# A table of attention biases written 16 times instead of 128, read by eight transfers, and compressor weights asked for in two pieces

## The chip, the cores and the metric

The kernel runs on one core of a Trainium2 chip. The metric is the time of one execution on the device in microseconds, the median of several runs. One further execution was recorded by the hardware profiler; its rows are shown below.

The core has a matrix engine (TensorE, PE in the rows, with its weight loads as PEld), VectorE (DVE), ScalarE (ACT), GpSimd (POOL) and SyncE (SP), and sixteen DMA engines that all transfers share. Each engine takes its instructions in order and waits on semaphores. SP, ACT and POOL also issue transfers; SP's and ACT's go through hardware queues (q1, q10 in the rows), POOL's through a software queue (q0).

## The reference

One layer of a block: normalise, project to many heads, two kinds of attention, project back, normalise, a feed-forward network. Only the part around the change is shown.

```
h = rms_norm(x, norm_mix_pre);  proj = h @ w_in            # x: 512 x 2048, all float32
k_cmp = compress_kv(kv6[:, :, 0], pe_k, w1_k, b1_k, w2_k)  # 31 blocks of 32 tokens, step 16
v_cmp = compress_kv(kv6[:, :, 1], pe_v, w1_v, b1_v, w2_v)
o_a = nsa_attention(q_a, k_cmp, v_cmp, k_slc, v_slc, k_win, v_win, gates, t5_bias)
o_r = silu(g_r) * retention(rope(q_r), rope(k_r), v_r)
x = x + rms_norm(concat(o_a, o_r) @ w_out);  x = x + rms_norm(square(relu(rms_norm(x) @ w_up)) @ w_down)

def compress_kv(kv, pe, w1, b1, w2):                       # w1: (32*128) x 128
    flat = (blocks of kv + pe).reshape(n_cmp, 32 * 128)
    return gelu(flat @ w1 + b1) @ w2
# in nsa_attention, for each of 8 heads, before each softmax:
s = q @ k.T * scale + t5_table[bucket(t_query - t_key), head]
```

The bias depends on the distance between query and key and on the head alone. So one row of 640 values for each head holds all of it, and the biases of query p are that row shifted by p places.

## The kernel before, in words

All products are made from two-part operands: ScalarE rounds a float32 tile to a high part (`whi`), VectorE subtracts to get the low part (`wlo`), and three matmuls (lines 154 to 156) add up. Weights come in slabs of 256 rows and up to 512 columns: SP asks for a slab (`raw`, line 175, three buffers), ScalarE casts it (line 143), VectorE subtracts (line 144), and TensorE uses it for 24 matmuls. There are three buffers for raw slabs and three for the two parts. Blocks of columns of `w_in` follow one another, eight slabs each: first the early value columns, then the **kv block** (the keys and values that are compressed), the **k block** (two transfers for each slab), the query block of the first group, and so on. `Driver.run` writes the casts of a slab two slabs ahead of its use, and its order in the program is the order on every engine.

Beside the products runs other work, cut into steps by generators: after some products `side.step()` takes one step of it. In the kv, k and first query blocks one step follows every second column group (`two`), so two for each slab. The first three units are `bias_table`, `compress(0)` for keys and `compress(1)` for values; the attention units (`nsa_unit`) of the first group follow from the fourth block on.

`bias_table` makes the table: two small matmuls give `rsb`, 8 heads on 8 partitions with 640 values each. POOL then writes it to DRAM as `rd`, with every head's row repeated 128 times (line 458). `load_bias` (line 551) reads it back for four heads of a group into `BT`: partition p takes row p at an offset of 127 - p, which gives the shift. One transfer does it, since a step of one row less one value moves on by a row and back by a place. The first load is written after the first query block, the second at the end of the first group's attention. `BT` is added to scores on VectorE (lines 572 and 582).

`compress(i)` asks on SP for the position rows `pes`, the bias `b1s`, `w2s` and the two halves of w1 (`w1s`, 16 x 128 x 128 values each, 1.05 MB, line 492); two steps later it transposes `pes` (L496), copies it beside the keys or values (`KV`, L497 on ScalarE), and runs 32 matmuls in four steps (L501): the first two read the first half of w1, the last two the second. The small transfers wait until the other compressor has read its own, since they share buffers.

Buffers are named by tags. `rsb`, `hot` and the two `KV` tiles share a tag with two buffers, so the third and fourth copies into `KV` (line 479) wait until the write of `rd` has read `rsb` to the end. `w1s` and `BT` share the tag `big`.

Of the kernel before, what the change touches and what calls it, by code (L numbers as in the profile page):

```python
# [10 lines left out]
F32 = mybir.dt.float32  # L11
# [5 lines left out]
P = 128  # L17
S = 512
# [4 lines left out]
HA, NG, DK = 8, 2, 128  # L23
# [3 lines left out]
EPS = 1e-6  # L27
KC = 2
NSLAB = KT // KC
RD = 639  # L30
LAST = 384

OFF_KV = HA * DK
# [79 lines left out]
def block_kernel(ctx: ExitStack, tc: tile.TileContext, x, norm_mix_pre, w_in, cmp_pe_k, cmp_w1_k, cmp_b1_k,  # L113
                 cmp_w2_k, cmp_pe_v, cmp_w1_v, cmp_b1_v, cmp_w2_v, t5_bias, w_out, norm_mix_post, norm_mlp_pre,
                 w_up, w_down, norm_mlp_post, c_rot, c_dec, c_hot, c_misc, out):
    nc = tc.nc
# [8 lines left out]
    dram = ctx.enter_context(tc.tile_pool(name="dram", bufs=1, space=bass.MemoryType.DRAM))  # L125
# [15 lines left out]
    def split(hi, lo, src):  # L141

        nc.scalar.copy(hi, src)  # L143
        nc.vector.tensor_sub(lo, src, hi.bitcast(F32))  # L144
# [18 lines left out]
    def bank(tag, bufs=1):  # L163
        return pp.tile([P, S], F32, name=tag, tag=tag, bufs=bufs)
# [140 lines left out]
    ap = actx.enter_context(tc.tile_pool(name="att", bufs=1))  # L305
# [140 lines left out]
    nc.gpsimd.dma_start(g3r, norm_mlp_pre.rearrange("o (k p) -> (o k) p", p=P))  # L446
    rot = rp.tile([P, 2, S], F32, name="rot")
    nc.gpsimd.dma_start(rot, c_rot)
    rd = dram.tile([HA, P, RD], F32, name="rd")

    def bias_table():
        rsb = ap.tile([HA, 640], F32, name="rsb", tag="P", bufs=2)
        for c0, n in ((0, 512), (512, 128)):
            ps = bank("S")
            nc.tensor.matmul(ps[:HA, :n], tbl, hot[:, c0:c0 + n], start=True, stop=True)
            nc.vector.tensor_copy(rsb[:, c0:c0 + n], ps[:HA, :n])
            yield
        nc.gpsimd.dma_start(rd, rsb[:, None, :RD].to_broadcast([HA, P, RD]))
        pt = bank("PT", 2)
        nc.tensor.transpose(pt[:, :KT], g3r, ident[:KT, :KT])  # L460
        nc.vector.tensor_copy(g3T, pt[:, :KT])
        yield
# [18 lines left out]
    def compress(i):  # L481
        pe, w1, b1, w2 = ((cmp_pe_k, cmp_w1_k, cmp_b1_k, cmp_w2_k), (cmp_pe_v, cmp_w1_v, cmp_b1_v, cmp_w2_v))[i]
        kv = KV[i]
        pes = ap.tile([CBLK, DK], F32, name="pes")
        nc.sync.dma_start(pes, pe[0])
        b1s = ap.tile([DK, 2], F32, name="b1s")
        nc.sync.dma_start(b1s[:, 0:1], b1.rearrange("o n -> n o"))
        w2s = ap.tile([DK, DK], F32, name="w2s")
        nc.sync.dma_start(w2s, w2[0])
        w1s = [ap.tile([P, 16, DK], F32, name="w1s", tag=("qT", "big")[c]) for c in range(2)]  # L490
        for c in range(2):
            nc.sync.dma_start(w1s[c], w1[0][c * 16 * P:(c + 1) * 16 * P, :].rearrange("(l p) n -> p l n", p=P))
        yield
        yield
        pt = bank("PT", 2)
        nc.tensor.transpose(pt[:, :CBLK], pes, ident[:CBLK, :CBLK])  # L496
        nc.scalar.copy(kv[:, NG * S:], pt[:, :CBLK])  # L497
        yield
        hid = bank("oT")
        for l in range(CBLK):  # L500
            nc.tensor.matmul(hid[:65, :DK], kv[:, l:l + STRIDE * 64 + 1:STRIDE], w1s[l // 16][:, l % 16, :],  # L501
                             start=l == 0, stop=l == CBLK - 1)
            if l % 8 == 7:
                yield
        hs = ap.tile([65, DK], F32, name="hs")
        nc.scalar.copy(hs, hid[:65, :DK])
        yield
        pt = bank("PT", 2)
        nc.tensor.transpose(pt[:, :65], hs, ident[:65, :65])
        nc.vector.tensor_add(b1s[:, 1:2], b1s[:, 0:1], pt[:, 64:65])  # L510
        z = ap.tile([DK, 4, 63], F32, name="z")
        nc.vector.tensor_scalar_add(z[:, 0, :], pt[:, :63], b1s[:, 1:2])

        nc.vector.tensor_mul(z[:, 1, :], z[:, 0, :], z[:, 0, :])
        nc.vector.tensor_scalar(z[:, 1, :], z[:, 1, :], 0.044715, 1.0, op0=ALU.mult, op1=ALU.add)
        nc.vector.tensor_mul(z[:, 1, :], z[:, 1, :], z[:, 0, :])
        nc.scalar.activation(z[:, 2, :], z[:, 1, :], AF.Exp, scale=-2.0 * float(np.sqrt(2.0 / np.pi)))
        yield
        nc.vector.tensor_scalar_add(z[:, 2, :], z[:, 2, :], 1.0)
        nc.vector.reciprocal(z[:, 2, :], z[:, 2, :])  # L520
        nc.vector.tensor_mul(z[:, 3, :], z[:, 0, :], z[:, 2, :])
        yield
        o = bank("PT", 2)
        if i == 0:
            nc.tensor.matmul(o[:, :63], w2s, z[:, 3, :], start=True, stop=True)
            for g in range(NG):
                nc.vector.tensor_copy(kS[:, g, :NCMP], o[:, g * 32:g * 32 + NCMP])
        else:
            for g in range(NG):
                nc.tensor.matmul(o[:NCMP, g * DK:(g + 1) * DK], z[:, 3, g * 32:g * 32 + NCMP], w2s,  # L530
                                 start=True, stop=True)
            split(vch, vcl, o[:NCMP, :NG * DK])
        yield

    QT, BT = {}, {}
# [12 lines left out]

    def load_bias(g):
        BT[g] = ap.tile([P, 4, S], F32, name="BT", tag="big")  # L550
        nc.gpsimd.dma_start(BT[g], bass.AP(tensor=rd.tensor, offset=rd.offset + g * 4 * P * RD + P - 1,
                                           ap=[[RD - 1, P], [P * RD, 4], [1, S]]))

    def nsa_unit(g, i, pr):

# [6 lines left out]
        def scores():  # L562
# [40 lines left out]
            if g == 0 and i == NT - 1 and pr == 1:  # L603
                load_bias(1)
# [170 lines left out]
    three = lambda c: side.step() if c else None  # L775
    after = lambda n: (lambda: drv.at > n * B)
    side.add(bias_table, nothing)
    side.add(lambda: compress(0), nothing, after(1))
    side.add(lambda: compress(1), nothing, after(1))
    for u in range(8):  # L780
        side.add(*nsa_unit(0, u // 2, u % 2), after(3), after(4))
# [7 lines left out]
    for blocks, units, firsts, pump in ((3, 3, 0, two), (4, 0, 0, two), (7, 10, 11, three), (8, 11, 12, three),  # L789
                                        (9, 12, 12, three), (10, 12, 19, two), (11, 19, 19, two),  # L790
                                        (12, 22, 22, three)):
        drv.run(blocks * B - 1, pump=pump)
        side.drain(units, firsts)
        if blocks == 3:
            load_bias(0)
        drv.run(blocks * B, pump=pump)
# [620 lines left out]
```

## Time and profile before

| what | value |
|---|---|
| median of 3 runs | 2289.46 us (2283.85 to 2302.96) |
| the profiled execution's own time | 2285.13 us |
| its span, first to last instruction | 2283.4 us |
| mean granted TensorE clock, share of full speed | 0.986 |
| TensorE matmul, busy | 2178.9 us (95%) |
| VectorE, busy | 1563.5 us (68%) |
| ScalarE, busy | 986.4 us (43%) |
| GpSimd, busy | 122.8 us (5%) |
| moved by DMA | 347.06 MB, mean 152 GB/s |

Busy times overlap, so they do not add up. A row of the timeline gives the start in us from the span's start, the duration, the engine, the line, the operation, and in brackets the engine's idle time just ahead of it with what ended it. A row of a window gives the busy time of each engine in that stretch with the count of instructions, then the granted clock, the share of the sixteen DMA engines and what they moved.

### The profile page before, as it was taken

The numbers are of one execution on the slowest core, as the hardware profiler recorded it, in microseconds if no ns is written. First come the engines' busy times: TensorE is split into PE (matmuls) and PEld (weight loads), VectorE is DVE, ScalarE is ACT, GpSimd is POOL, SyncE is SP. The second block draws the span as 40 slices with busy tenths as digits, with TensorE's granted clock in tenths as the row PEclk, the third lists the DMA queues.
The fourth block names the chain that finished last, engine by engine and source line by source line (L and its number), as shares of the span: only waits on it lengthen the run. The fifth ranks groups of instructions, "written<-read, shape, count | busy, mean of one in ns | idle before, by whom it ended". The sixth has DMA issues, their size and how long they took to land.

```text
span 2283.4 us, 31751 instructions
## 1 busy us (share of the span) xinstructions
PE 2178.9 (95%) x12787; PEld 1917.7 (84%) x12787; DVE 1563.5 (68%) x1868; ACT 986.4 (43%) x1432; POOL 122.8 (5%) x133
## 2 busy tenths in 40 slices
PE   8799999999999999999999999999899999999994
PEld 7578878888788899888999999999778888888873
DVE  6122556554655633488877888888768998899897
ACT  5022344243232323475545555555554444444442
POOL 0000000000000000000000000000000000000002
PEclk9899999999999999999999999999999999999997
DMA  6552323322223334477767676767565656566655
GB/s 191 88 155 88 111 64 94 93 76 81 78 86 119 106 105 136 143 247 192 211 176 204 191 196 179 195 179 205 183 230 162 206 157 204 156 200 177 183 150 83
DMA packets 252661, 347.06 MB, mean 152 GB/s; under 512 B 14331, under 2 KB 164171, under 8 KB 251873
## 3 DMA queue, kind: packets, MB, share of 16 engines
q1 hardware_dynamic: 212000, 288.23, 39.1%
q0 software_dynamic: 30416, 45.25, 12.5%
q10 hardware_dynamic: 10098, 11.55, 1.5%
q8 instruction: 100, 1.64, 0.3%
q14 instruction: 47, 0.39, 0.0%
HBM read 300.95 MB, written 44.04 MB: 151 GB/s over the span
## 4 chain that ended last, share of the span: by engine, by line
PE 74%; DVE 11%; DMA 6%; ACT 3%; issue 3%; POOL 1%; SPq 0%; ACTq 0%; POOLq 0%; DVEq 0%
PE prod L155 13%; PE prod L156 13%; PE prod L154 12%; PE mm L154 10%; PE mm L156 10%; PE mm L155 10%; DVE wlo L927 4%; DMA raw<-in_w_in 3%; DMA Y<-in_w_up 2%; DVE Hl L144 2%; PE S L581 2%; ACT whi L951 1%; DVE low L947 1%; DVE Y L947 1%; DVE acc L1313 1%
## 5 line engine op out<-in xcount | busy, mean ns | idle before, releaser
L951 ACT CAST whi<-Y 128x1024 fp32r<-128x1024 f32 x228 | 238.4, 1049 | 305.5 <-DVE Y L947 116.1
L155 PE MATMUL prod<-wlo,Hh 128*128 128x512 f32 x896 | 352.3, 393 | 18.1 <-DVE wlo L927 18.1
L144 DVE TENSOR_TENSOR wlo<-raw,whi 128x1024 fp32r<-128x1024 f32 (+4 forms) x152 | 168.4, 1113 | 283.2 <-ACT whi L143 272.1
L154 PE MATMUL prod<-whi,Hh 128*128 128x512 f32 x896 | 348.9, 389 | 0.0
L156 PE MATMUL prod<-whi,Hl 128*128 128x512 f32 x896 | 348.8, 389 | 0.0
L951 ACT CAST whi<-low 128x1024 fp32r<-128x1024 f32 x214 | 224.4, 1052 | 278.0 <-DVE low L947 102.9
L927 DVE TENSOR_TENSOR wlo<-Y,whi 128x1024 fp32r<-128x1024 f32 x228 | 277.6, 1221 | 60.4 <-ACT whi L951 58.8
L156 PE MATMUL prod<-Hh,wlo 128*128 128x256 f32 x1024 | 284.9, 278 | 11.8 <-DVE wlo L927 11.8
L927 DVE TENSOR_TENSOR wlo<-low,whi 128x1024 fp32r<-128x1024 f32 x214 | 260.7, 1221 | 51.6 <-ACT whi L951 49.9
L143 ACT CAST whi<-raw 128x1024 fp32r<-128x1024 f32 (+4 forms) x152 | 145.5, 960 | 331.6 <-PE mm L155 126.5
L154 PE MATMUL prod<-Hh,whi 128*128 128x256 f32 x1024 | 284.3, 278 | 4.4 <-DVE Y L822 4.4
L155 PE MATMUL prod<-Hl,whi 128*128 128x256 f32 x1024 | 283.6, 277 | 0.0
L154 PE MATMUL mm<-whi,Hh 128*128 128x416 f32 (+4 forms) x704 | 262.8, 373 | 1.4 <-ACT Hh L143 1.4
L156 PE MATMUL mm<-whi,Hl 128*128 128x416 f32 (+4 forms) x704 | 248.4, 353 | 0.7 <-DVE Hl L144 0.7
L155 PE MATMUL mm<-wlo,Hh 128*128 128x416 f32 (+4 forms) x704 | 247.9, 352 | 0.0
L154 PE MATMUL mm<-Hh,whi 128*128 128x512 f32 x512 | 218.0, 426 | 16.7 <-ACT whi L143 10.8
L155 PEld LDWEIGHTS prod<-wlo,Hh 128*128 128x128 f32 x896 | 168.1, 188 | 65.0 <-DVE wlo L927 30.8
L156 PE MATMUL prod<-sx,wlo 128*128 128x256 f32 x768 | 214.0, 279 | 6.7 <-DVE wlo L927 6.7
L154 PE MATMUL prod<-sx,whi 128*128 128x256 f32 x768 | 213.8, 278 | 1.4 <-ACT whi L951 1.4
L155 PE MATMUL prod<-sx,whi 128*128 128x256 f32 x768 | 213.5, 278 | 0.0
L156 PEld LDWEIGHTS prod<-Hh,wlo 128*128 128x128 f32 x1024 | 193.0, 188 | 14.2 <-DVE wlo L927 14.2
L156 PE MATMUL mm<-Hh,wlo 128*128 128x512 f32 x512 | 203.1, 397 | 0.1
(289 smaller groups left out, 3965.7 us busy)
## 6 DMA issues: line engine op xcount, KB each, us to landing
raw<-in_w_in SPq DMA_DIRECT2D x160, 256.0 KB, 3.1
low<-in_w_up SPq DMA_DIRECT2D x38, 1024.0 KB, 6.1
Y<-in_w_up SPq DMA_DIRECT2D x32, 1024.0 KB, 6.1
low<-in_w_down SPq DMA_DIRECT2D x32, 1024.0 KB, 5.2
Y<-in_w_down SPq DMA_DIRECT2D x32, 1024.0 KB, 5.2
Y<-ud SPq DMA_DIRECT2D x49, 512.0 KB, 8.6
ud<-Y SPq DMA_DIRECT2D x73, 256.0 KB, 4.6
raw<-in_w_out SPq DMA_DIRECT2D x32, 416.0 KB, 3.4
```

Of the source, the lines that this page charges most:

```text
L143: nc.scalar.copy(hi, src)
L144: nc.vector.tensor_sub(lo, src, hi.bitcast(F32))
L154: nc.tensor.matmul(ps, ah, bh, start=first, stop=False)
L155: nc.tensor.matmul(ps, ah, bl, start=False, stop=False)
L156: nc.tensor.matmul(ps, al, bh, start=False, stop=last)
L581: nc.tensor.matmul(sps[:, :c + L], QT[g][:, h, qs], k, start=True, stop=True)
L927: nc.vector.tensor_sub(lo, src, hi.bitcast(F32))
L947: nc.vector.tensor_add(to, to, by)
L951: nc.scalar.copy(hi, src)
L1313: nc.vector.tensor_add(e[p], ps, e[p])
```

## The change

The table is written 16 times instead of 128, in rows of 640 values instead of 639. Eight transfers then read it for each group, each for 16 partitions: for partition p0 + p the row p at the offset 127 - p0 - p. In `compress` a step ends after each half of w1, where before both were asked for in one step and two empty steps followed; the number of steps is the same.

```diff
-RD = 639
+RD = 640
...
-    rd = dram.tile([HA, P, RD], F32, name="rd")
+    RB = 16
+    rd = dram.tile([HA, RB, RD], F32, name="rd")
...
-        nc.gpsimd.dma_start(rd, rsb[:, None, :RD].to_broadcast([HA, P, RD]))
+        nc.gpsimd.dma_start(rd, rsb[:, None, :].to_broadcast([HA, RB, RD]))
...
         for c in range(2):
             nc.sync.dma_start(w1s[c], w1[0][c * 16 * P:(c + 1) * 16 * P, :].rearrange("(l p) n -> p l n", p=P))
-        yield
-        yield
+            yield
...
         BT[g] = ap.tile([P, 4, S], F32, name="BT", tag="big")
-        nc.gpsimd.dma_start(BT[g], bass.AP(tensor=rd.tensor, offset=rd.offset + g * 4 * P * RD + P - 1,
-                                           ap=[[RD - 1, P], [P * RD, 4], [1, S]]))
+        for p in range(0, P, RB):
+            nc.gpsimd.dma_start(BT[g][p:p + RB], bass.AP(
+                tensor=rd.tensor, offset=rd.offset + g * 4 * RB * RD + P - 1 - p,
+                ap=[[RD - 1, RB], [RB * RD, 4], [1, S]]))
```

On SP, at the end of the k block, the order before is this; `raw_1080` is the last slab of the k block, `raw_1125` and `raw_1158` the first two of the query block.

```order
L175 DMA raw_1080<-in_w_in 128x2x256 [waits DMAHW1_49,DMAHW0_49,DVE_49]
L175 DMA raw_1080<-in_w_in 128x2x256
L485 DMA pes_1115<-in_cmp_pe_v 32x128 [waits PE_49]
L487 DMA b1s_1117<-in_cmp_b1_v 128x1 [waits DVE_49]
L489 DMA w2s_1119<-in_cmp_w2_v 128x128 [waits DMAHW2_49,PE_49]
L492 DMA w1s_1121<-in_cmp_w1_v 128x16x128 [waits DMAHW3_49]
L492 DMA w1s_1122<-in_cmp_w1_v 128x16x128 [waits DMAHW4_49]
L175 DMA raw_1125<-in_w_in 128x2x512 [waits DMAHW5_49,Activation_49]
L175 DMA raw_1158<-in_w_in 128x2x512 [waits DMAHW6_49,Activation_49]
```

Now the first query slab (`raw_1124`) stands between the two halves of w1:

```order
L490 DMA w2s_1119<-in_cmp_w2_v 128x128 [waits DMAHW2_49,PE_49]
L493 DMA w1s_1121<-in_cmp_w1_v 128x16x128 [waits DMAHW3_49]
L175 DMA raw_1124<-in_w_in 128x2x512 [waits DMAHW4_49,Activation_49]
L493 DMA w1s_1122<-in_cmp_w1_v 128x16x128 [waits DMAHW5_49]
L175 DMA raw_1158<-in_w_in 128x2x512 [waits DMAHW6_49,Activation_49]
```

So one half moved past one slab. For the keys the two halves stay side by side, because no slab is asked for between those two steps.

On POOL, from the constants to the first retention head, the order before is this; `rot` and `dec` are constants of the other kind of attention.

```order
L448 DMA rot<-in_c_rot 128x1024 [waits PE_49]
L458 DMA rd<-rsb 1024x1x639 [waits DVE_49]
L551 DMA BT<-rd 128x4x512 [waits DMAHW2_49,DMAHW4_49,DMAHW1_49,DMAHW5_49,DMASW5_49,PE_49]
L551 DMA BT<-rd 128x4x512 [waits DMASW6_49,DVE_49]
L697 DMA dec<-in_c_dec 128x512 [waits DMASW0_49]
```

And now:

```order
L448 DMA rot<-in_c_rot 128x1024 [waits PE_49]
L459 DMA rd<-rsb 128x1x640 [waits DVE_49]
L552 DMA BT<-rd 16x4x512 [waits DMAHW2_49,DMAHW1_49,DMAHW5_49,DMASW5_49,PE_49]
L552 DMA BT<-rd 16x4x512
L552 DMA BT<-rd 16x4x512 [waits DMASW0_49]
L552 DMA BT<-rd 16x4x512 [waits DMASW1_49]
L552 DMA BT<-rd 16x4x512 [waits DMASW2_49]
L552 DMA BT<-rd 16x4x512 [waits DMASW3_49]
L552 DMA BT<-rd 16x4x512 [waits DMASW4_49]
L552 DMA BT<-rd 16x4x512
L552 DMA BT<-rd 16x4x512 [waits DMASW4_49,DMASW3_49,DMASW5_49,DMASW2_49,DMASW6_49,DMASW1_49,DMASW7_49,DMASW0_49,DVE_49]
L552 DMA BT<-rd 16x4x512 x7
```

Each load became eight transfers of 16 partitions, and `dec` (now line 699) stands behind the second eight.

## Rows read from the trace of the kernel before

**Rows 1.** The page, busy us of an engine, share of the span, instructions.
```profile
PE 2178.9 (95%) x12787; PEld 1917.7 (84%) x12787; DVE 1563.5 (68%) x1868; ACT 986.4 (43%) x1432; POOL 122.8 (5%) x133
```

**Rows 2.** Windows: busy us of each engine (instructions), granted clock, DMA share, GB/s.
```profile
57.00:84.00 27.00, 27.00 (x119) 21.76 (x117) 3.62 (x4) 2.09 (x2) 0.89 (x1) 1.00 0.58 85
84.00:127.00 43.00, 26.25 (x87) 19.37 (x86) 6.13 (x5) 7.72 (x10) 0.00 (x0) 0.76 0.71 152
...
168.00:177.00 9.00, 6.97 (x34) 6.00 (x34) 2.45 (x2) 4.09 (x7) 0.00 (x0) 0.81 0.74 239
...
158.00:170.00 12.00, 10.15 (x44) 7.77 (x43) 0.00 (x0) 1.00 (x2) 0.00 (x0) 1.00 0.97 283
```

**Rows 3.** Timeline of TensorE, 83 to 127 us.
```profile
88.51 0.80 PE L154 MATMUL mm<-Hh,whi 128*128 128x512 f32 x1 [4.46 <-ACT whi L143]
...
102.88 0.79 PE L154 MATMUL mm<-Hh,whi 128*128 128x512 f32 x1 [6.29 <-ACT whi L143]
...
116.58 0.79 PE L154 MATMUL mm<-Hh,whi 128*128 128x512 f32 x1 [5.92 <-ACT KV L479]
...
126.78 0.24 PE L496 MATMUL PT<-misc,pes 32*128 32x32 f32 x1
```

**Rows 4.** Timeline of ScalarE, 60 to 172 us.
```profile
87.41 1.04 ACT L143 CAST whi<-raw 128x1024 fp32r<-128x1024 f32 x1 [18.83 <-DMA raw<-in_w_in]
...
115.95 2.04 ACT L479 COPY KV<-mm 128x512 f32<-128x512 f32 x4
...
169.00 1.04 ACT L143 CAST whi<-raw 128x1024 fp32r<-128x1024 f32 x1 [14.20 <-DMA raw<-in_w_in]
169.95 0.18 ACT L497 COPY KV<-PT 128x32 f32<-128x32 f32 x1
```

**Rows 5.** Timeline of POOL, 0 to 375 us.
```profile
56.80 1.09 POOL L458 DMA_DIRECT2D rd<-rsb  x1 [6.69 <-DVE rsb L456]
187.87 0.80 POOL L551 DMA_DIRECT2D BT<-rd  x1 [129.98 <-PE oT L501]
369.11 0.76 POOL L551 DMA_DIRECT2D BT<-rd  x1 [180.44 <-DVE Pt L582]
369.87 0.55 POOL L697 DMA_DIRECT2D dec<-in_c_dec  x1
```

**Rows 6.** DMA, 57 to 113 us: packets, MB, share; KB each, median us to landing.
```profile
q0 software_dynamic: 1040, 2.62, 44.9%
...
rd<-rsb POOLq DMA_DIRECT2D x1, 2556.0 KB, 55.9
...
raw<-in_w_in SPq DMA_DIRECT2D x2, 512.0 KB, 33.3
```

**Rows 7.** DMA issues of the whole kernel, same columns.
```profile
raw<-in_w_in SPq DMA_DIRECT2D x24, 512.0 KB, 4.4
...
BT<-rd POOLq DMA_DIRECT2D x2, 1024.0 KB, 6.1
```

**Rows 8.** Timeline of TensorE, 168 to 187 us.
```profile
170.18 2.53 PE L501 MATMUL oT<-w1s,KV 128*65 128x128 f32 x16 [2.03 <-ACT KV L497]
...
176.45 1.97 PE L501 MATMUL oT<-w1s,KV 128*65 128x128 f32 x16
...
181.01 1.98 PE L501 MATMUL oT<-w1s,KV 128*65 128x128 f32 x16
```

**Rows 9.** Timeline of SP, 156 to 161 us.
```profile
157.36 2.90 SPq L492 DMA_DIRECT2D w1s<-in_cmp_w_v  x2
160.37 3.28 SPq L175 DMA_DIRECT2D raw<-in_w_in  x1
```

**Rows 10.** Timeline of VectorE: first reads of BT, and of dec (402.25).
```profile
228.46 0.28 DVE L582 SCALAR_TENSOR_TENSOR Pt<-S,BT 128x128 f32<-128x128 f32 x1
...
402.25 0.69 DVE L706 TENSOR_TENSOR AT<-S,dec 128x512 f32<-128x512 f32 x1 [2.37 <-PE S L704]
...
443.30 0.29 DVE L582 SCALAR_TENSOR_TENSOR Pt<-S,BT 128x128 f32<-128x128 f32 x1 [0.20 <-PE S L581]
```

## The prediction

> **What bounds the kernel now.** I read the page first: TensorE is busy 95% of the span [rows 1], so a change that touches only transfers can win time only where TensorE stands still or runs at its lower clock. The windows show where that is near the change. From 57 to 84 us TensorE has no gap: 27.00 us for 119 matmuls, 0.227 us each, at a granted clock of 1.00. From 84 to 127 it is busy 26.25 of 43.00 us at a mean granted clock of 0.76, and from 168 to 177 it is busy 6.97 of 9.00 at 0.81 [rows 2]. 1.00 is the level of 2.4 GHz; the two means are mixtures of it with 1.2 GHz, to which the clock falls after each pause. The TensorE timeline gives the pauses of the first stretch: 4.46, 6.29 and 5.92 us, the first two for a cast of a weight slab, the third for a copy of KV [rows 3]. ScalarE's timeline says what those casts wait for: at 87.41 it had stood 18.83 us for a transfer of raw weights, and the KV copies at 115.95 stand behind such casts in its order [rows 4]. The transfers of that stretch explain why the weights are late. POOL issues the write of rd at 56.80 [rows 5], and it takes 55.9 us for 2,556 KB; while it runs, a 512 KB weight transfer takes a median of 33.3 us, against 4.4 over the whole kernel, and rd's queue holds 44.9% of sixteen engines, about 7.2 of them [rows 6, 7]. So the first loss is the table's write.
>
> The second loss is smaller and elsewhere. At 170.18 the compressor's matmul (L501) waits 2.03 us for the small KV copy L497 [rows 8]. That copy needs only a transpose, but on ScalarE it stands behind a cast that had waited 14.20 us for raw weights [rows 4]. On SP that weight transfer is issued at 160.37, right behind both halves of the value compressor's w1, whose issues run from 157.36 for 2.90 us [rows 9].
>
> **The change part by part.** *The table's write.* It falls from 1,024 rows of 2,556 B to 128 of 2,560 B, one eighth. By its own row 55.9 / 8 = 7.0 us. The bounds are far apart: at the 283 GB/s of the stretch 158 to 170 [rows 2] the 0.33 MB take 1.2 us, and if the cost did not go by bytes it would stay at 55.9. I take 7.0, because the row is the same transfer from the same eight partitions. The write then lands near 65 us instead of 113.
>
> What was late must now be in time. TensorE ends its sixth kv slab at 88.51 - 4.46 = 84.05. The seventh needs its cast to begin by about 82.9 (in the trace 1.10 us lie between cast and matmul, 87.41 to 88.51), and its raw transfer is asked for near 58, when the raw buffer comes free. Held up until 65 and then given the usual 4.4 us, it lands near 70, 13 us early. The write could take 21 us before it costs anything. A second condition is less strict: the third KV copy goes into the buffer that rsb held, so it waits for the write to land; its product ends 42 matmuls after 84.05, near 94.
>
> The gain: from 84.05 to the transpose L496 at 126.78 lie 42.73 us, and in them 24 + 24 + 36 = 84 matmuls (two kv slabs, one and a half of the next block). At 0.227 us they take 19.1, so the stretch gives back 23.6. It checks: the three pauses are 16.67, and the other 7 us are matmuls at half pace after each. Next in line is the key compressor's w1, 2.1 MB on SP ahead of the weights for slab 4 of the next block. In the new kernel SP reaches it when the buffer for slab 2 has been asked for, after the fifth kv slab ends near 78.6 and a cast, so near 81 to 84 us; at 283 GB/s it needs 7.4 us, and the slab behind it lands near 94, while its cast is due only when slab 0 ends, at 84.05 + 72 x 0.227 = 100.4. I cost that at nothing; the cover is those 6 us, and if it fails the price is like the second loss below.
>
> *The w1 in two pieces.* On SP one slab transfer now stands between the halves of the value compressor's w1; for the key compressor nothing moves, since no slab is asked for between the two steps. In the trace both halves and the slab, 2 x 1.05 + 0.52 MB, are through when the cast starts at 169.00. With 1.05 MB less ahead of it the slab lands 1.05 / 0.283 = 3.7 us sooner, near 165.3. The matmul L501 starts 1.18 us after that cast begins, so to follow without a pause at 168.15 the cast must begin by 166.97: 1.7 us to spare. The second half lands when the slab did, near 169 to 170 in the old time, and is first read at 181.01. The gain is the pause of 2.03 us and the half pace behind it: from 170.18 to 176.45 are 6.27 us for the same sixteen L501 and twelve matmuls that take 4.56 from 176.45 to 181.01 [rows 8]. That is 2.03 + 1.71 = 3.7.
>
> *The table's read in eight pieces.* It adds seven issues on POOL for each of two loads. The issue of one whole load is 0.80 us; a piece has an eighth of its rows, so 0 to 0.80 each, and I take the upper end: 6.4 us, and 6.1 for the last to land, as long as a whole load takes [rows 7]. The first load starts at 187.87 [rows 5] and is read at 228.46, the second at 369.11 and 443.30 [rows 10]: the last pieces land near 200 and 382. Behind the second load on POOL stands dec, issued at 369.87, which slips by under 6 us; it is read at 402.25. VectorE's first read now waits on eight pieces instead of one transfer, and all are long done. Cost nothing.
>
> This is where the Trainium skill speaks against the change: DMA: Bandwidth & Descriptors, section "Rules for kernel authors", says that splitting a transfer over groups of partitions gains nothing, since the pieces share the same engines, and that many small transfers should be made one large one. By the fit in its section "Anatomy of one DMA" (about 2.0 us each plus the bytes at 436 GB/s) eight pieces one after another would be an estimated 18 us; by that the sum is the same, as 40 us lie free.
>
> **The sum.** 23.6 + 3.7 = 27.3 us. The rest of the kernel shifts as it is, since everything after waits on TensorE's progress. The profiled execution took 2285.13 us (span 2283.4 and 1.7 around it): 2257.8. That execution is 4.3 below the median of the three runs, from which the same gain gives 2262.2. I say 2260.
>
> **The rivals.** *One compressor load still stalls TensorE.* The slab now between the halves keeps only 1.7 us to spare, and SP's own issue of it took 3.28 us behind w1 [rows 9], which may be the queue filling; the key compressor's 6 us could fail too. For it: the same order made the stall. Against: 1.05 MB less ahead. Then the gain is 27.3 - 3.7 = 23.6, and the time 2263.6.
>
> *The write is not cheaper by bytes.* If the cost lay in reading from eight partitions or in a fixed part, rd could still take over 21 us, and up to 55.9. Against: it is one transfer whose rows are of one kind. At 55.9 the first term is gone and only 3.7 stays: 2284; that is the change not doing what it says.
>
> *Slower: the pieces come too late.* If pieces followed one another at a latency of their own, the first scores would wait. From 187.87 to 228.46 are 40.6 us, so eight pieces hurt from 5.1 us each; at the 6.1 us that a whole load takes to land, eight need 48.8, a wait of 8, and the gain is 19. Slower than before needs more than 27.3 + 40.6 = 67.9 us, 8.5 us for each piece; at 10 us each the first load ends 39.4 late and the second 5.8, together 45.2: 2260 + 45.2 = 2305. Against: no piece waits for the one ahead of it in the program, and 10 us is more than any row of such a transfer shows, apart from the table's write.
>
> **How the numbers follow.** The forecast has 0.70, the stalling load 0.18, the dear write 0.06, the late pieces on the slower side 0.02, and 0.04 is left for other times near the forecast. The range holds the first two: 2257.8 and 2263.6 with about 7 us on either side, for the runs of the kernel before alone lie 19 us apart: 2251 to 2271. About 1% (22.9 us) is what a measurement of this kernel can tell from no change. 27.3 is 1.2% and 23.6 just over 1%, so a little noise takes either under the line: faster by over 1% is 0.8 of the forecast, half of the stalling case and half of the rest, 0.67; within 1% 0.30; slower 0.03.
>
> **What would show it.** In the changed kernel rd should land within some 7 us; TensorE should have no pause between 57 us and the end of the value compressor, at a granted clock of 1.00; L496 should come first near 103, and the second L496 should be followed by L501 without a wait; the first read of BT should not wait on a transfer. Wrong would be: rd in flight past 80 us, a cast waiting for raw weights behind either w1, or VectorE waiting for BT.

## The result, and the profile after

The kernel after took 2261.36 us (median of 4 runs, 2258.81 to 2271.72), the kernel before on the same chip 2295.42 (4 runs): a ratio of 0.9875, 95% interval 0.9838 to 0.9912. (The two medians alone would give 0.9852: two of the four runs of before took over 2301 us, so the median of so few is a rough figure.) The profiled executions have spans of 2261.9 us after and 2283.4 before, 21.5 apart.

The page's row of the engines first; it answers to [rows 1].

```profile
PE 2175.6 (96%) x12787; PEld 1919.0 (85%) x12787; DVE 1563.7 (69%) x1868; ACT 986.9 (44%) x1432; POOL 129.1 (6%) x147
```

TensorE does the same 12787 matmuls in 2175.6 us, 3.3 less than before. The other 18.2 of the 21.5 are idle time that is gone, near the sum of the four pauses, 16.67 [rows 3] and 2.03 [rows 8]. The windows of the kernel after show where, in the columns of [rows 2]. The third is the value compressor, which before lay at 168 to 177.

```profile
57.00:84.00 27.00, 27.00 (x120) 21.62 (x119) 6.59 (x7) 5.24 (x5) 0.62 (x1) 1.00 0.40 93
84.00:127.00 43.00, 43.00 (x222) 36.46 (x221) 7.36 (x6) 9.95 (x13) 0.00 (x0) 1.00 0.43 124
142.00:152.00 10.00, 10.00 (x60) 8.52 (x59) 2.45 (x2) 4.77 (x8) 0.00 (x0) 1.00 0.88 281
```

From 84 to 127 TensorE now does 222 matmuls where it did 87 (64 of the 222 are the short ones of L501, which before came only after 127), with no gap, at a granted clock of 1.00 (2.4 GHz) where the mean was 0.76. Its timeline after, against [rows 3, 8]:

```profile
104.71 0.24 PE L496 MATMUL PT<-misc,pes 32*128 32x32 f32 x1
...
142.88 0.24 PE L496 MATMUL PT<-misc,pes 32*128 32x32 f32 x1
...
145.92 1.98 PE L501 MATMUL oT<-w1s,KV 128*65 128x128 f32 x16
...
150.49 1.98 PE L501 MATMUL oT<-w1s,KV 128*65 128x128 f32 x16
```

The first L496 comes at 104.71 instead of 126.78, and L501 at 145.92 has no wait in brackets. The DMA issues from 50 to 100 us, against [rows 6]. The 0.5 KB of `w1s` is not the size of a half, which is 1.05 MB:

```profile
q0 software_dynamic: 288, 0.85, 9.7%
...
rd<-rsb POOLq DMA_DIRECT2D x1, 320.0 KB, 8.2
w1s<-in_cmp_w_k SPq DMA_DIRECT2D x2, 0.5 KB, 7.8
```

One 512 KB weight transfer is issued while the write runs, at 59.72. Its row, from 59 to 66 us, and the row of the same transfer of before, from 57 to 63 us:

```profile
raw<-in_w_in SPq DMA_DIRECT2D x1, 512.0 KB, 8.3
```

```profile
raw<-in_w_in SPq DMA_DIRECT2D x1, 512.0 KB, 29.3
```

The write takes 8.2 us instead of 55.9, and the weight transfer beside it 8.3 instead of 29.3; the next one, issued when the write is all but through, takes 4.3. So ScalarE's cast in that stretch now waits for TensorE to free the buffer that it writes, not for a transfer. In the value compressor a cast still waits 10.73 us for its slab, but ends in time (ScalarE's timeline, against [rows 4]):

```profile
85.55 1.05 ACT L143 CAST whi<-raw 128x1024 fp32r<-128x1024 f32 x1 [4.39 <-PE mm L155]
...
143.46 1.05 ACT L143 CAST whi<-raw 128x1024 fp32r<-128x1024 f32 x1 [10.73 <-DMA raw<-in_w_in]
144.41 0.18 ACT L497 COPY KV<-PT 128x32 f32<-128x32 f32 x1
```

SP's timeline shows the slab between the halves, against [rows 9]:

```profile
135.29 0.72 SPq L493 DMA_DIRECT2D w1s<-in_cmp_w_v  x1
136.11 1.91 SPq L175 DMA_DIRECT2D raw<-in_w_in  x1
138.23 0.71 SPq L493 DMA_DIRECT2D w1s<-in_cmp_w_v  x1
```

POOL's timeline has the pieces, against [rows 5], and VectorE's the first reads of BT and dec, against [rows 10]:

```profile
58.50 0.62 POOL L459 DMA_DIRECT2D rd<-rsb  x1 [6.69 <-DVE rsb L457]
...
161.92 4.07 POOL L552 DMA_DIRECT2D BT<-rd  x8 [102.79 <-PE oT L501]
...
343.19 4.05 POOL L552 DMA_DIRECT2D BT<-rd  x8 [177.20 <-DVE Pt L584]
347.23 0.57 POOL L699 DMA_DIRECT2D dec<-in_c_dec  x1
```

```profile
202.50 0.28 DVE L584 SCALAR_TENSOR_TENSOR Pt<-S,BT 128x128 f32<-128x128 f32 x1
...
376.33 0.69 DVE L708 TENSOR_TENSOR AT<-S,dec 128x512 f32<-128x512 f32 x1 [2.37 <-PE S L706]
...
417.39 0.29 DVE L584 SCALAR_TENSOR_TENSOR Pt<-S,BT 128x128 f32<-128x128 f32 x1 [0.20 <-PE S L583]
```

Eight issues take POOL 4.05 us, and no read of BT or dec waits for a transfer.

**Where the time came from.** One number is used below for every kernel: the time from the write's issue to the second group's first read of BT ("to the second group's read"). Gains in it are against this first trace of before; a second trace, below, gives 2.1 us less. Before it is 443.30 - 56.80 = 386.50 us, after 417.39 - 58.50 = 358.89: a gain of 27.6. At its end the gain in the span is 21.5. Of the 6.1 between, 1.7 are lost before the write (it is issued at 58.50 instead of 56.80, in a stretch that the change doesn't touch), and 4.4 behind 417 us, nearly all of it between 1030 and 1137 us, in the first blocks of w_up. A second trace of the kernel before (below) lost 1.5 us against the first in the same place, so a part of this is a difference between executions. More than that, in the twelve traces of this document the matmuls there (the 4,000th to the 6,000th of the kernel) take from 299.5 us (sixteen partitions) to 307.6 us (32 copies), against 300.0 before and 304.1 after, and the kernels that have pauses in the first stretch and those that have none overlap. So nothing ties the 4.4 us to the change.

### The profile page after: what moved, and what is told of

The parts are those of the page before. It is cut to its first block, busy times and chain, and to the rows that moved or that the text cites. A ratio compares the mean times of both kernels' runs of the same rounds, so it can differ in the third digit from the quotient of the medians.

```text
span 2261.9 us, 31774 instructions
## 1 busy us (share of the span) xinstructions
PE 2175.6 (96%) x12787; PEld 1919.0 (85%) x12787; DVE 1563.7 (69%) x1868; ACT 986.9 (44%) x1432; POOL 129.1 (6%) x147
## 4 chain that ended last, share of the span: by engine, by line
PE 77%; DVE 12%; DMA 4%; ACT 3%; issue 3%; POOL 1%; SPq 0%; ACTq 0%; POOLq 0%; DVEq 0%
PE prod L155 13%; PE prod L156 13%; PE prod L154 13%; PE mm L154 11%; PE mm L156 10%; PE mm L155 10%; DVE wlo L929 4%; DMA Y<-in_w_up 2%; DVE Hl L144 2%; PE S L583 2%; ACT whi L953 1%; DVE low L949 1%; DVE Y L949 1%; DVE acc L1315 1%; DMA low<-in_w_up 1%
```

## The experiments

The theory: the gain is the sum of two separate pauses, the one made by the write because it holds its DMA engines in proportion to its rows, the other by SP's order around the value compressor's w1; the eight pieces cost nothing because their end lies far ahead of every reader. The rivals: the two parts need each other; the write is dear for another reason (its rows' 2,556 bytes, POOL's software queue); the pieces have a price that something hides. Each kernel starts from the kernel after, unless it is said to be the kernel before with one thing changed. Where only one run was made, it stands beside one run or more of the kernel before on the same chip.

**The table alone** (both halves of w1 asked for together, as before):

```diff
-            yield
+        yield
+        yield
```

> The table part alone: written 16 times, read by eight transfers, w1 still asked for in one step. My theory: TensorE has no pause from 57 us to the first L496, which comes about 23.6 us sooner than in the kernel before; the value compressor keeps its pause of about 2 us and the half pace behind it. So 23.6 us of the 27.3, in time some 2262 to 2266 if the kernel before takes 2285 to 2290, ratio 0.990. Rival, the two parts need each other: then far less than 23 us. Rival, the whole gain is the table's: then 27 us, and no pause at the value compressor.

Measured 2263.82 us (4 runs), ratio 0.9889 (0.986 to 0.9919). To the second group's read the gain is 23.9. TensorE is busy all of both windows, 57 to 84 and 84 to 127, and the small pause stands where it stood (TensorE's and ScalarE's timeline of this kernel):

```profile
146.56 2.90 PE L502 MATMUL oT<-w1s,KV 128*65 128x128 f32 x16 [1.85 <-ACT KV L498]
```

```profile
145.38 1.04 ACT L143 CAST whi<-raw 128x1024 fp32r<-128x1024 f32 x1 [14.01 <-DMA raw<-in_w_in]
```

The cast waits 14.01 us for its slab, against 10.73 in the kernel after, and L502 (L501 of the others) waits 1.85 behind it. From the write to the first L496 this kernel takes 46.21 us, as the kernel after does. The large term belongs to the table's part alone.

**The w1 alone** (table as before: 128 copies of 639, one read):

```diff
-RD = 640
+RD = 639
-    RB = 16
-    rd = dram.tile([HA, RB, RD], F32, name="rd")
+    rd = dram.tile([HA, P, RD], F32, name="rd")
...
-        for p in range(0, P, RB):
-            nc.gpsimd.dma_start(BT[g][p:p + RB], bass.AP(
+        nc.gpsimd.dma_start(BT[g], bass.AP(tensor=rd.tensor, offset=rd.offset + g * 4 * P * RD + P - 1,
```

> The w1 part alone: the table is written 128 times and read by one transfer as before, the second half of w1 is asked for a step later. My theory: the three pauses of the first stretch stay (about 16.7 us), the pause of 2.03 us at the value compressor goes with the half pace behind it, so the fourth step of L501 comes 3.7 us sooner against the first L496 than before; ratio 0.998, which the timing can hardly tell from 1. Rival: the slab between the halves still comes late, and the distance stays as it was.

Measured 2285.65 us (12 runs), ratio 0.9992 (0.9975 to 1.001): no difference that the timing shows, and one of 0.16% would lie inside that interval. The trace does show it: 4.05 us gained to the second group's read, no wait at L501, and the three large pauses in place, in its TensorE timeline:

```profile
88.85 0.50 PE L154 MATMUL mm<-Hh,whi 128*128 128x512 f32 x1 [4.17 <-ACT whi L143]
...
103.18 0.80 PE L154 MATMUL mm<-Hh,whi 128*128 128x512 f32 x1 [6.22 <-ACT whi L143]
117.16 0.80 PE L154 MATMUL mm<-Hh,whi 128*128 128x512 f32 x1 [6.22 <-ACT KV L479]
```

The parts add: 23.9 + 4.05 = 27.95 against 27.6 for both; how firm the 4.05 is, the next run tells. Its span, 2296.0, is longer than that of before for a reason of its own, told at the end.

**The kernel before again**, for the size of what no edit makes.

> The kernel before once more, for a second trace of it. The kernel after had won 26 us by 990 us, but only 21.5 by the end: 1.7 us were lost ahead of 38 us and 4.4 between 1035 and 1140. If these are the difference between two executions, this trace will differ from the first by 1 to 4 us in the same places. If they belong to the change, it will match the first trace there within some 0.3 us.

Measured 2285.67 us, span 2283.9. The pauses are 4.16, 6.33 and 6.15 us, with a small one of 0.53 behind the first. L501 waits 1.80 us, the write is issued 1.1 us later than in [rows 5], and 1.5 us are lost between 1030 and 1066 us. So the three large pauses and that of L501 repeat to 0.3 us, and one to two microseconds at the start and near 1030 come and go without an edit.

One thing does not repeat. Here is TensorE's timeline at the value compressor, to be held against [rows 8], and the window from 172 to 175, of the first trace and then of this one:

```profile
170.73 2.09 PE L501 MATMUL oT<-w1s,KV 128*65 128x128 f32 x16 [1.80 <-ACT KV L497]
...
175.42 1.98 PE L501 MATMUL oT<-w1s,KV 128*65 128x128 f32 x16
```

```profile
172.00:175.00 3.00, 3.00 (x10) 2.50 (x9) 0.64 (x1) 0.35 (x1) 0.00 (x0) 0.50 0.78 199
```

```profile
172.00:175.00 3.00, 3.00 (x19) 2.57 (x18) 1.19 (x1) 1.48 (x3) 0.00 (x0) 1.00 0.60 175
```

In the first trace the granted clock was 0.50 (1.2 GHz) behind the pause, in this one it stayed at 1.00 (2.4 GHz), and the first step of L501 with the matmuls behind it took 4.69 us instead of 6.27. So this trace takes 442.31 - 57.90 = 384.41 us to the second group's read, 2.1 less than the first, and against it the gains are 25.5 for the kernel after, 21.9 for the table alone and 2.0 for the w1 alone. By stretches the parts separate without this blur:

| kernel | from the write to the first L496, us | from the second L496 to the second step of L501, us |
|---|---|---|
| before, first trace | 69.98 | 11.50 |
| before, second trace | 69.66 | 9.70 |
| the w1 alone | 69.80 | 7.61 |
| the table alone | 46.21 | 11.31 |
| after | 46.21 | 7.61 |

What remains up to the second group's read is 305.0 to 305.1 us in all five. So the table is worth 23.5 to 23.8 us, and the w1 2.1 to 3.9, by whether the clock falls behind the pause that it removes.

**The table written 64 times, and 32 times** (read by two transfers and by four):

```diff
-    RB = 16
+    RB = 64
```

> The kernel after, but the table written 64 times and read by two transfers of 64 partitions. My theory, the write costs by its bytes on the engines that it holds: it lands about 28 us after its issue (half of 55.9), near 86, past the 21 us that I said were free; the seventh kv slab comes about as late as before, for a pause of some 4 to 5 us with 2 us of half pace behind it, and no second or third pause; 6 to 7 us more than the kernel after. Rival, a fixed cost of such a write that sixteen rows happen to escape: all three pauses, 23 us more. Rival, half the write is free: no pause.

> The kernel after, but the table written 32 times and read by four transfers of 32 partitions. By bytes the write lands about 14 us after its issue, inside the 21 us that I said were free: TensorE has no pause, and the time is that of the kernel after. Rival, the free stretch is smaller than I worked out: a pause ahead of the seventh kv slab.

Measured 2264.59 and 2263.79 us. With 64 copies the gain is 21.3, with 32 it is 27.65, that of the kernel after. The write's rows from the DMA issues, 64 copies and then 32:

```profile
rd<-rsb POOLq DMA_DIRECT2D x1, 1280.0 KB, 28.6
```

```profile
rd<-rsb POOLq DMA_DIRECT2D x1, 640.0 KB, 14.9
```

14.9 us cost TensorE nothing, 28.6 us cost one pause, in the timeline with 64 copies:

```profile
87.01 0.80 PE L154 MATMUL mm<-Hh,whi 128*128 128x512 f32 x1 [2.76 <-ACT whi L143]
```

The point lies between 14.9 and 28.6, as the 21 us of the prediction have it. The pause is smaller than the expectation said, 2.76, but with the matmuls behind it at the lower clock (granted 0.50 from 87 to 93 us, which is 1.2 GHz) the loss is 6.3, within the 6 to 7 that it named. The write now has five sizes: 1.9 us for 8 rows (below), 8.2 for 128, 14.9 for 256, 28.6 for 512 and 55.9 for 1,024. From 128 and 1,024 rows, (55.9 - 8.2) / 896 = 53 ns a row and 1.4 us fixed; that line gives 1.8, 15.0 and 28.6 for the other three. The 1,024 rows were of 2,556 bytes and the others of 2,560, so the row's length plays no part.

**128 copies, sent from sixteen partitions.** The table is computed twice, on sixteen partitions instead of eight, and each sends 64 rows; the rest is the kernel before.

```diff
+    tbl = ap.tile([33, HA, 2], F32, name="tbl")
...
-        rsb = ap.tile([HA, 640], F32, name="rsb", tag="P", bufs=2)
+        rsb = ap.tile([2 * HA, 640], F32, name="rsb", tag="P", bufs=2)
+        nc.vector.tensor_copy(tbl, tb8[:, :, None].to_broadcast([33, HA, 2]))
...
-        nc.gpsimd.dma_start(rd, rsb[:, None, :].to_broadcast([HA, RB, RD]))
+        nc.gpsimd.dma_start(rd.rearrange("h (a r) n -> (h a) r n", a=2), rsb[:, None, :RD].to_broadcast([2 * HA, P // 2, RD]))
```

> The kernel before with its 128 copies, but the table's rows lie twice in SBUF, on 16 partitions, and each partition writes 64 copies. If the write runs on as many engines as the source has partitions (8 of 16 before, by the share of 44.9%), it now runs on 16 and lands after about 28 us instead of 55.9, with a share near 90% while it runs, and the first stretch loses some 7 to 10 us instead of 23.6. If it is the bytes written to DRAM that set its time, it stays near 56 us and all three pauses stay.

Measured 2279.94 us; the gain to the second group's read is 18.2. From its DMA issues, 57 to 87 us:

```profile
q0 software_dynamic: 528, 2.62, 81.8%
...
rd<-rsb POOLq DMA_DIRECT2D x1, 2556.0 KB, 28.6
```

The same bytes land in 28.6 us instead of 55.9, and in the same 30 us of the kernel before the queue held 45.3% of sixteen engines: 13.1 engines against 7.2. So the write was long because it was sent from eight partitions. The Trainium skill, DMA: Bandwidth & Descriptors, section "Why a DMA increments its semaphore by 16 and not by 1", says that a transfer is spread over the largest number of engines, up to 16, that divides the slowest dimension of both its sides; these two shares fit, a little under eight and under sixteen. That the number of engines sets the pace is not shown, since this kernel doubles the partitions together with the engines. The write moved 2.62 MB in 55.9 us on 7.2 engines, 6.5 GB/s each, while in the window from 158 to 170 of [rows 2] sixteen engines moved 283 GB/s, some 18 each: the engines that the write held did not run at what they can do, and the few partitions that they read may be the reason. Even so, fewer copies are the better cure: one pause of 2.77 us stays here, as with 64 copies, whose write lasts as long (28.6 us for half of the bytes). So that pause goes with the time for which the write runs, not with its bytes. The first stretch loses 5.5 us against the kernel after, less than the 7 to 10 of the expectation.

**128 copies, sent from ScalarE's hardware queue** instead of POOL's; the rest is the kernel before.

```diff
-        nc.gpsimd.dma_start(rd, rsb[:, None, :].to_broadcast([HA, RB, RD]))
+        nc.scalar.dma_start(rd, rsb[:, None, :RD].to_broadcast([HA, P, RD]))
```

> The kernel before, but ScalarE's hardware queue issues the write of the table (128 copies, 8 partitions) instead of POOL's software queue. If the time lies in the engines that the write holds, it lands after some 56 us again and the pauses stay. If the software queue is what is slow, it lands sooner, by half or more, and the pauses shrink.

Measured 2287.19 us, beside 2290.55 of before. Its queue in the DMA view, 50 to 125 us, and the pause in TensorE's timeline:

```profile
q10 hardware_dynamic: 1032, 2.62, 31.8%
```

```profile
114.73 0.80 PE L154 MATMUL mm<-Hh,whi 128*128 128x512 f32 x1 [18.16 <-ACT KV L479]
```

The trace doesn't tell when this write lands, but it takes as much of the engines: 31.8% of 75 us is 23.9 us of sixteen, and 44.9% of 56 us in [rows 6] is 25.1. The three pauses have become one of 18.16 (and 0.73 us in two small ones), before the copy of KV that takes the table's buffer; their sum was 16.67. L496 comes at 125.21, against 126.78 [rows 3]. So POOL's software queue was not the cause; what the engines carry was.

**The table written once**, each load read by 128 pieces of one partition. It puts the price of a piece where it can be seen.

```diff
-    RB = 16
+    RB = 1
```

> The kernel after, but the table written once and read by 128 transfers of one partition for each group. The kernel after showed 0.51 us of POOL for each piece. If that holds for a piece of one partition, the first load takes 66 us of POOL from about 162, past the first read near 202: VectorE and then TensorE wait some 30 us; the second has 74 us and is in time, but dec stands behind it on POOL and comes near 413 instead of 347, and is read near 376 plus the first delay, so little or no wait there. So 30 to 36 us more than the kernel after, slower than the kernel before by 4 to 15 us. Rival, a piece of one partition costs in proportion to its rows: a few us of POOL in all, no wait, the time of the kernel after. Rival, pieces follow one another at their latency of some 6 us: hundreds of us more.

Measured 2338.19 us, 77 above the kernel after, some 14 of them from the slower w_up stage told at the end: slower than before, and by more than was expected. A piece lands in 1.9 us but holds POOL for 0.50, so a load is issued in 65 us, from 160.85 to 225.9 and from 369.42 to 435.4. In VectorE's timeline the first scores wait, and so does dec, for which little or no wait was expected:

```profile
227.52 0.29 DVE L584 SCALAR_TENSOR_TENSOR Pt<-S,BT 128x128 f32<-128x128 f32 x1 [26.00 <-DMA BT<-rd]
...
438.79 0.69 DVE L708 TENSOR_TENSOR AT<-S,dec 128x512 f32<-128x512 f32 x1 [38.59 <-DMA dec<-in_c_dec]
```

The time to the second group's read is 65.1 us longer than after. The second load's own reader never waited: dec, issued behind its pieces on POOL, is wanted first.

**The same, with the first dec asked for on SP.**

```diff
-            nc.gpsimd.dma_start(dec, c_dec[:, h, :])
+            (nc.gpsimd if h else nc.sync).dma_start(dec, c_dec[:, h, :])
```

> Table written once and read by 128 pieces a load, as in the run before it of that form, but the first dec is asked for on SP's queue instead of POOL's, so it no longer stands behind the second load's 128 issues. Theory (the slow form lost about 26 us at the first scores and 38 at dec, because dec is queued behind the pieces): the wait of 38.59 us for dec is gone; the wait of about 26 us at the first read of BT stays; the second load is through by about 436 and its first read comes only near 443, so nothing there. At the second group's first read the kernel stands 25 to 29 us behind the kernel after, about level with the kernel before: 2288, up to 2303 if the w_up stage runs in its slower pace. Rival (the 38 us are the second load's own, by its issues or transfers holding something else that the first retention head needs): a wait of 20 us or more stays there and the time is 2310 or more.

Measured 2307.82 us (6 runs), ratio to before 1.0075 (1.0051 to 1.0099). Between the two expectations, nearer the rival's: dec is read at 401.19 without a wait for it, but half of the 38 us stays, for the next thing in POOL's order (VectorE's timeline):

```profile
415.22 0.43 DVE L743 BATCH_NORM_STATS2 rst<-oT 128x6 f32<-128x256 f32 x1 [1.08 <-PE oT L741]
...
435.25 0.54 DVE L747 TENSOR_SCALAR rn<-oT,rst 128x256 f32<-128x256 f32 x1 [19.19 <-POOL rst L161]
```

L161 is the retention's inverse root, a 0.55 us operation that runs on POOL; it starts at 434.63, when the last piece is issued. TensorE stands 17.91 us behind it. Against the kernel after this one is 47.5 us late at the second group's read, 17.5 less than with dec on POOL.

**The table written twice**, 64 pieces a load:

```diff
-    RB = 16
+    RB = 2
```

> Table written twice, read by 64 pieces a load. Theory (a piece costs POOL 0.50 us, and what decides is the end of the issues): the first load is issued from 162 to 194 and read at 202, no wait; the second from 343 to 375.5, then dec, which lands near 378 and is wanted at 376.3: a wait of 1 to 4 us for dec. Gain to the second group's first read 24 to 27 us against 27.6 with 16 copies; 2262 to 2268. Rival (cost goes with the number of pieces wherever they stand): about half of what 128 pieces cost, 33 us, is lost: about 2294. A margin of 8 us at the first read may be less if pieces of two rows take longer than those of one.

Measured 2272.96 us (6 runs), ratio 0.9931 (0.9901 to 0.996): still faster than before, 11.6 slower than after. To the second group's read it is 13.0 behind; the expectation had 1 to 4. POOL's and then VectorE's timeline:

```profile
378.97 3.23 POOL L552 DMA_DIRECT2D BT<-rd  x6 [2.76 <-issue]
382.19 0.59 POOL L699 DMA_DIRECT2D dec<-in_c_dec  x1
```

```profile
385.57 0.69 DVE L708 TENSOR_TENSOR AT<-S,dec 128x512 f32<-128x512 f32 x1 [12.79 <-DMA dec<-in_c_dec]
```

The place was right, the price too low: a piece of two partitions takes POOL 0.547 us, and POOL also stood between pieces, some of the time for earlier pieces to land, so the second load is issued in 40.2 us (342.01 to 382.19) instead of 32. The first load, from 160.76 to 196.13, is read at 201.34 without a wait.

## Why the prediction was right

*The table's write, 7.0 us.* It took 8.2: an eighth of the rows' part, 6.8, and 1.4 that are fixed, which a plain eighth of 55.9 divides too. It lands at 66.7, and since 21 us were free (14.9 cost nothing, 28.6 cost a pause) the error has no effect. The 21 are themselves a little small. They give a slab 4.4 us to land once the write is through, but in the kernel after it lands 1.3 us behind the write, and with 64 copies 0.2 (issued at 58.22, 27.6 us in flight). From that run an estimate is 28.6 - 2.76, some 26 us.

*The gain of 23.6.* From the write's issue to L496, 126.78 - 56.80 = 69.98 before and 104.71 - 58.50 = 46.21 after: 23.8; the table alone has the same 46.21. Against the second trace of before it is 23.5. This is the step on which the result rests, and it holds, with no pause and a clock of 1.00.

*The key compressor's w1, costed at nothing.* SP issues it at 84.99, or 83.3 in the old time (81 to 84 was said). The 7.8 us of its row are the median of two halves; the second lands near 95.3, so the 2.1 MB took some 10 us and not 7.4. The slab behind it lands near 96.8, or 95.1 in the old time (94), and its cast begins at 101.87, when TensorE has freed a buffer: some 5 us were to spare where 6 were said, and TensorE has no gap through 127.

*The w1 in two pieces, 3.7.* The mechanism holds in every trace: the pause at L501 is gone in all seven that have this part and stands in all five that don't. The size is half luck. Alone it gave 4.05 against the first trace of before; in the kernel after L501's second step comes at 150.49 instead of 176.45, 25.96 sooner, of which 22.07 were won by L496: 3.9. But 1.7 of the 3.7 are matmuls at half pace, and the prediction has the clock fall "after each pause". The second trace of before has the pause without the fall, and there the part is worth 2.1. The slab's cast begins at 143.46, which is 165.5 in the old time (165.3 was said), inside the margin of 1.7. The rival that doubted this had SP's issue of 3.28 us [rows 9] for it; alone between the halves it took 1.91.

*The pieces, 0 to 0.80 us each.* 0.51, and landing in 6.6 (6.1): the first load is through near 173, 11 us after its first issue, since the pieces overlap, and read at 202.50. Nothing waits. The rival on the slower side was not met, but its point was put in the wrong place: it counted the delay of BT's readers alone, 5.1 us a piece to hurt at all. The prediction saw dec behind the second load and let it slip "by under 6 us", without asking from when that costs. The runs with 64 and 128 pieces show that dec is late first, and the inverse root behind it. In the kernel after the second load's issues could grow from 4.05 us to an estimated 24 to 30 (from 343.19 to 376.33 are 33.1, less 3.3 us for dec to land, as with 128 pieces, to 8.9, as in the kernel after), 3.0 to 3.7 us a piece, before dec is late.

*The write is not cheaper by bytes.* Sending from eight partitions does limit the write, as that rival had it, but it halves the rate against sixteen and leaves the cost in proportion to the rows.

*The sum, 27.3.* 27.6 to the second group's read, from the trace that the sum was worked from; 25.5 from the second trace of before. "The rest of the kernel shifts as it is" is the step least borne out: the span of this one execution keeps 21.5. The ratio of the timed runs, 0.9875 of 2295.42, is 28.7 us (20 to 37), which holds both. 2260 was forecast and 2261.36 came, but the four runs of the kernel after lie 12.9 us apart, so that these two meet to 1.4 us is luck.

## What to carry to other kernels

A store that repeats a few partitions' rows many times holds the few DMA engines that those partitions give it, and its price is paid by other transfers: look for weight loads that take several times their usual time, and ask how long the store may take before the first of them is late, since shortening it further is worth nothing (32 copies gain what 16 do). When a transfer is cut into pieces, price the issues on the queue's engine, and then find everything that stands behind them there, operations as well as transfers; the first reader that is late is often not the reader of the pieces. Where two parts of a change touch separate waits, a kernel with one part alone shows each term, and a trace can show a pause of 2 us gone that twelve timed runs can't. Take a second trace of the kernel before as well: what the pause cost behind it differed by 1.6 us between two executions of one program.

## What the runs showed of the hardware

Pauses of nearly the same length at L501 were followed by different clocks. Behind 2.03, 1.85 and 1.82 us (before, the table alone, sixteen partitions) the granted clock was about 0.5 (1.2 GHz) for some 3 us; behind 1.80 and 2.02 us (before again, ScalarE's queue) it stayed at 1.00 (2.4 GHz). What decides this, no run shows.

In three traces (the w1 alone, sixteen partitions, the table written once) the w_up stage ran at a slower pace: from 1273 to 1578 us of the kernel before lie eight blocks of 336 matmuls, and these took 39.57 us each instead of 38.08. With the stretches beside them it was 13 to 15 us in all, with the same program there. The windows of one block, of the kernel before and then of the w1 alone:

```profile
1434.00:1472.00 38.00, 38.00 (x337) 38.00 (x337) 30.94 (x32) 21.13 (x26) 2.54 (x2) 1.00 0.68 187
```

```profile
1439.00:1479.00 40.00, 40.00 (x342) 40.00 (x341) 31.43 (x32) 21.60 (x27) 2.61 (x3) 1.00 0.65 179
```

And the groups of instructions in the same two windows (count, busy us, mean ns of one):

```profile
L154 PE MATMUL prod<-Hh,whi 128*128 128x256 f32 x65 | 17.9, 276 | 0.0
```

```profile
L154 PE MATMUL prod<-Hh,whi 128*128 128x256 f32 x66 | 18.5, 281 | 0.0
```

TensorE is busy throughout, with no wait and a granted clock of 1.00 in both, yet each matmul takes 281 ns instead of 276 (they overlap: one starts every 118 ns instead of 113). The size agrees with the spread of the timed runs of before (2285 to 2301). What causes it stays open; no run here was aimed at it. It is why a single span of such a kernel can't be read to better than some 15 us, and why the time to the second group's read was used here.
